# All 256 tokens turned before the first product, fp32r products as filler on TensorE, and high-part products first in the opening passes of a short-convolution layer

## The chip, the cores and the metric

The kernel runs on one core of one Trainium2 chip. The metric is the device time of one execution in microseconds (us), as the median of several runs. The engines are TensorE (PE; its weight loads are PEld), VectorE (DVE), ScalarE (ACT), GpSimd (POOL) and SyncE (SP), which issues most of the DMAs.

## What is computed

One layer for 256 tokens of width 2048, with a branch width of 4096, all in float32:

```python
h = rmsnorm(x, norm_g[0])                      # (1, 256, 2048)
mod = silu(c) @ ada_w[0] + ada_b[0]            # (1, 6144): shift, scale, gate
h = h * (1.0 + scale) + shift
proj = h @ w_in                                # (1, 256, 16384)
b_gate, c_gate, v, g = split(proj, 4)
u = causal_depthwise_conv(c_gate * v, conv_w)  # width 3
y = (b_gate * u * silu(g)) @ w_out             # (1, 256, 2048)
out = rmsnorm(x + gate * y, final_g)
```

The weights are large against the activations: `w_in` has 134 MB, `ada_w` 50 MB, `w_out` 34 MB, and each is read once.

## The kernel before, in words

**Precision.** A float32 product is made of three fp32r products: every operand is split into a high part (a cast to fp32r) and a low part (the rest), and high x high, high x low and low x high are added in PSUM. For a piece of `w_in` the split is a CAST `hi` on ACT (line 335) and a subtraction `lo` on DVE (line 336). For the features it is `hT`: its high half `hh_` is written on ACT (325), its low half `hl_` on DVE (326 and 329). The three products of a weight block are called 0 (hi, `hh_`), 1 (hi, `hl_`) and 2 (lo, `hh_`) in `product` (line 430 issues them all).

**Order of the input projection.** The 2048 input features are 16 slices k of 128. Features can be used only once their `shift` and `scale` are known, and these need all 16 rows of a piece of `ada_w`, so slices come in groups of two (`ADA = [2] * 8`). `plan()` writes down the order of the work: passes over a pair of 512-column chunks and one of four quarters of `w_in`, each with a range k0 to k1 of slices. The first passes use slices 0 and 1 alone (the opening passes, k0 = 0); later ones add more slices to the saved partial sums `acc`. A pass of 2 chunks and 2 slices loads 1 MB of `w_in`, is 48 products, and has one or two pieces of `ada_w` of 512 KB beside it. In this text P0 and P1 are the two first, half-wide passes (24 products each), and P2, P3 and so on are the passes behind them in the plan's order; the eighth opening pass, P8, takes slices 0 to 3. SP loads in the order of the plan: `raw_s` (line 478, three buffers) and `at` (399, four buffers). A finished bank goes to `acc` (451 on ACT, or 453 on DVE); a later pass may begin with a copy of `acc` back into its bank (465, a seed).

**The front.** `in_order()` pins the order on every engine, as traced, from the loads of `x` up to `pinned.close()`. x is loaded as four tiles `x00`, `x01`, `x10`, `x11` (128 tokens x 1024 columns). ACT and DVE make the sums of squares, `rstd` follows (281 to 283). `turn_x(0, 4)` scales the first 512 columns of x (ACT, 296 and 300), turns them on PE (eight transposes, 305) and copies them to `xs` on ACT (306). The first piece of `ada_w` (16 rows k, `first_ada`) is summed with `silu_c`: rows 7, 11 and 15 on PE (`ON_PE`, four products of 128 x 1 each, line 348), the others on DVE into `gv0` (359, 361), which a last product with ones adds up (`sum0(None, ...)`). `idle(n)` fills PE's waits with `IDLE` transposes of the identity matrix (251). `modulate` then makes `scale` and `shift` (320 to 322) and the features of slices 0 and 1.

**Behind the front.** The other twelve slices of x are turned in the middle of the opening passes: `turn_at` calls `turn_x` after the fourth, sixth and tenth saved partial sum, and with the first of these the convolution's weights are turned too (`turn(rows2, ...)`). In every chunk the products run block by block, with all three terms of a block together: high, high, low (`chunk_products`); the two first half-wide pieces alone go term by term (`late=True`). Outside the pinned front a scheduler places the instructions by its own estimate of time, so the order on an engine isn't the order of the code alone.

Of the kernel before, what the change touches and what calls it, by code (L numbers as in the profile page):

```python
# [8 lines left out]
F32 = mybir.dt.float32  # L9
F32R = mybir.dt.float32r  # L10
# [3 lines left out]
P = 128  # L14
D = 2048
E = 4096
T = 256
# [111 lines left out]
def short_conv_layer(ctx: ExitStack, tc: tile.TileContext, x, c, norm_g, ada_w, ada_b, w_in, conv_w, w_out, final_g, out):  # L129
# [69 lines left out]
    IDLE = (16, 30, 24, 14, 14, 6)  # L199
# [14 lines left out]
    for n, (j, kk) in enumerate(((0, 4), (4, 4), (8, 4), (12, 2), (14, 1), (15, 1))):  # L214
# [4 lines left out]
        if j == KT - 1:  # L219
            raw0 = raw_tile("raw0")  # L220
            first_load(raw0, 0)
# [3 lines left out]
    for k in range(1, NK0):  # L225
        first_load(raw0, k)
# [20 lines left out]
    tp_idle = psum.tile([P, CT, T], F32, tag="mm", name="tp_idle")  # L247

    def idle(n):
        for _ in range(n):  # L250
            nc.tensor.transpose(tp_idle[:, 0, 0:P], ident, ident)


# [4 lines left out]
    idle(IDLE[0])  # L258
# [4 lines left out]
    idle(IDLE[1])  # L263
# [15 lines left out]
    nc.vector.tensor_copy(vec, tp_v)  # L279
    nc.vector.tensor_scalar_add(b_scale1, vec[:, 32:48], 1.0)  # L280
# [11 lines left out]
    def turn_x(k0, k1, vector=False):  # L292

        c0, n = k0 % 8 * P, (k1 - k0) * P
        x0, x1 = (xt[t][k0 // 8][:, c0 : c0 + n] for t in range(TT))
        nc.scalar.activation(x0, x0, AF.Copy, scale=rstd[:, 0:1])
        if vector:
            nc.vector.tensor_scalar_mul(x1, x1, rstd[:, 1:2])
        else:
            nc.scalar.activation(x1, x1, AF.Copy, scale=rstd[:, 1:2])  # L300
        for i in range(0, k1 - k0, 2):
            tp = psum.tile([P, 2, T], F32, tag="sm", name="tp_x", bufs=2)
            for j in range(2):
                for t, xn in enumerate((x0, x1)):
                    nc.tensor.transpose(tp[:, j, t * P : (t + 1) * P], xn[:, (i + j) * P : (i + j + 1) * P], ident)  # L305
            nc.scalar.copy(xs[k0 // CT][:, k0 % CT + i : k0 % CT + i + 2, :], tp)
# [4 lines left out]
    def modulate(k0, nk, sums):  # L311
# [11 lines left out]
        for k in range(k0, k0 + nk):  # L323
            hf = xs[k // CT][:, k % CT, :]
            nc.scalar.activation(hh_[:, k], hf, AF.Identity, bias=shift[:, k : k + 1], scale=scale[:, k : k + 1])  # L325
            nc.vector.tensor_scalar(
                out=hf, in0=hf, scalar1=scale[:, k : k + 1], scalar2=shift[:, k : k + 1], op0=ALU.mult, op1=ALU.add
            )
            nc.vector.tensor_tensor(out=hl_[:, k], in0=hf, in1=hh_[:, k].bitcast(F32), op=ALU.subtract)
# [397 lines left out]
```

## Time and profile before

| | |
|---|---|
| median of 3 runs | 922.97 us (922.72 to 924.28) |
| profiled execution | 922.73 us |
| its span, first to last instruction | 921.0 us |
| around the span | 1.7 us |
| mean granted TensorE clock | 0.994 |
| PE busy | 905.1 us, 98% |
| DVE busy | 627.0 us, 68% |
| ACT busy | 450.3 us, 49% |
| moved by DMA | 227.64 MB, mean 247 GB/s |

A row of the timeline shows the start in us from the span's start, the length in us, the engine, the line, the operation, what it writes and reads, its shape and the number of instructions that were merged into it; in brackets stands the idle time of the engine before it, and who ended that. A row of the windows shows the length of a stretch and, for each engine, its busy time with the number of instructions, then the granted TensorE clock (1.00 is full), the busy share of the DMA engines and GB/s. The chain of waits is followed back from the last instruction to what released each step; its rows are start, length and what ran.

### The profile page before, as it was taken

The numbers are of one execution on the slowest core, as the hardware profiler recorded it, in microseconds if no ns is written. First come the engines' busy times: TensorE is split into PE (matmuls) and PEld (weight loads), VectorE is DVE, ScalarE is ACT, GpSimd is POOL, SyncE is SP. The second block draws the span as 40 slices with busy tenths as digits, with TensorE's granted clock in tenths as the row PEclk, the third lists the DMA queues.
The fourth block names the chain that finished last, engine by engine and source line by source line (L and its number), as shares of the span: only waits on it lengthen the run. The fifth ranks groups of instructions, "written<-read, shape, count | busy, mean of one in ns | idle before, by whom it ended". The sixth has DMA issues, their size and how long they took to land.

```text
span 921.0 us, 16348 instructions
## 1 busy us (share of the span) xinstructions
PE 905.1 (98%) x7119; PEld 871.3 (95%) x7119; DVE 627.0 (68%) x601; ACT 450.3 (49%) x427; POOL 0.7 (0%) x6
## 2 busy tenths in 40 slices
PE   7899999999999999999999999999999999999996
PEld 7899999999999999999999999999999988888885
DVE  5888898999875899986545544555454535555882
ACT  3778975545544755544443334433444333443333
POOL 0000000000000000000000000000000000000000
PEclk9899999999999999999999999999999999999999
DMA  9999999999995569867566656665666486565542
GB/s 313 368 382 357 344 336 360 342 348 344 353 347 200 184 214 353 276 209 229 186 200 200 192 185 194 203 198 184 191 188 201 142 330 229 192 205 195 184 137 91
DMA packets 147367, 227.64 MB, mean 247 GB/s; under 512 B 5424, under 2 KB 103904, under 8 KB 146912
## 3 DMA queue, kind: packets, MB, share of 16 engines
q1 hardware_dynamic: 147056, 226.51, 73.2%
q8 instruction: 55, 0.90, 0.4%
q10 hardware_dynamic: 240, 0.09, 0.0%
q14 instruction: 16, 0.13, 0.0%
HBM read 224.49 MB, written 2.10 MB: 246 GB/s over the span
## 4 chain that ended last, share of the span: by engine, by line
PE 95%; DMA 3%; SPq 1%; DVE 0%; ACT 0%; ACTq 0%; issue 0%; DVEq 0%
PE mm_b L430 38%; PE mm_s L430 37%; PE mm_o L625 6%; PE mm_o L626 6%; PE mm_o L624 6%; DMA at<-in_ada_w_dram 2%; DMA x<-in_x_dram 1%; DMA raw_s<-in_sc_w_in_dram 1%; PE ps_gate L563 0%; SPq L223 0%; PE tp_g L419 0%; PE tp_x L305 0%; DVE lo L336 0%; SPq L203 0%; SPq L399 0%; ACT big L643 0%
## 5 line engine op out<-in xcount | busy, mean ns | idle before, releaser
L430 PE MATMUL mm_s<-hT,hi 128*128 128x256 f32 x2048 | 353.0, 278 | 1.0 <-ACT hT L325 0.5
L430 PE MATMUL mm_b<-hT,hi 128*128 128x256 f32 x2048 | 348.8, 276 | 0.0
L430 PEld LDWEIGHTS mm_s<-hT,hi 128*128 128x128 f32 x2048 | 310.6, 189 | 2.1 <-ACT hT L325 0.7
L430 PEld LDWEIGHTS mm_b<-hT,hi 128*128 128x128 f32 x2048 | 308.3, 188 | 0.2 <-issue 0.2
L430 PE MATMUL mm_s<-hT,lo 128*128 128x256 f32 x1024 | 283.1, 278 | 1.8 <-DVE lo L336 1.8
L430 PE MATMUL mm_b<-hT,lo 128*128 128x256 f32 x1024 | 282.6, 276 | 0.0
L336 DVE TENSOR_TENSOR lo<-raw,hi 128x2048 fp32r<-128x2048 f32 (+1 forms) x66 | 148.0, 2243 | 128.1 <-ACT hi L335 128.1
L335 ACT CAST hi<-raw 128x2048 fp32r<-128x2048 f32 (+1 forms) x66 | 123.7, 1874 | 203.8 <-PE mm_b L430 149.9
L430 PEld LDWEIGHTS mm_s<-hT,lo 128*128 128x128 f32 x1024 | 192.9, 189 | 2.0 <-DVE lo L336 2.0
L430 PEld LDWEIGHTS mm_b<-hT,lo 128*128 128x128 f32 x1024 | 192.2, 188 | 0.2 <-issue 0.2
L335 ACT CAST hi<-raw_s 128x2048 fp32r<-128x2048 f32 (+1 forms) x64 | 121.6, 1901 | 102.6 <-PE mm_s L430 88.9
L336 DVE TENSOR_TENSOR lo<-raw_s,hi 128x2048 fp32r<-128x2048 f32 (+1 forms) x64 | 145.4, 2273 | 33.2 <-ACT hi L335 30.3
L336 DVE TENSOR_TENSOR lo<-raw_o,hi 128x2048 fp32r<-128x2048 f32 x32 | 73.3, 2291 | 66.1 <-ACT hi L335 66.1
L335 ACT CAST hi<-raw_o 128x2048 fp32r<-128x2048 f32 x32 | 61.0, 1907 | 106.9 <-PE mm_o L626 88.0
L625 PE MATMUL mm_o<-lo,y 128*128 128x512 f32 x256 | 99.7, 391 | 0.0
L624 PE MATMUL mm_o<-hi,y 128*128 128x512 f32 x256 | 99.3, 389 | 0.0
L626 PE MATMUL mm_o<-hi,y 128*128 128x512 f32 x256 | 99.3, 389 | 0.0
L412 DVE SCALAR_TENSOR_TENSOR gv<-at,silu_c,gv 128x512 f32<-128x512 f32 x105 | 78.5, 749 | 2.5 <-DMA at<-in_ada_w_dram 0.8
L625 PEld LDWEIGHTS mm_o<-lo,y 128*128 128x128 f32 x256 | 48.1, 188 | 10.1 <-issue 0.2
L626 PEld LDWEIGHTS mm_o<-hi,y 128*128 128x128 f32 x256 | 48.0, 188 | 10.1 <-issue 0.2
L624 PEld LDWEIGHTS mm_o<-hi,y 128*128 128x128 f32 x256 | 48.1, 188 | 10.0
L451 ACT COPY acc<-mm_s 128x1024 f32<-128x1024 f32 x43 | 43.5, 1014 | 18.1 <-PE mm_s L430 18.0
(94 smaller groups left out, 382.2 us busy)
## 6 DMA issues: line engine op xcount, KB each, us to landing
raw<-in_sc_w_in_dram SPq DMA_DIRECT2D x64, 1024.0 KB, 5.6
raw_s<-in_sc_w_in_dram SPq DMA_DIRECT2D x63, 1024.0 KB, 7.0
raw_o<-in_sc_w_out_dram SPq DMA_DIRECT2D x32, 1024.0 KB, 5.2
at<-in_ada_w_dram SPq DMA_DIRECT2D x114, 256.0 KB, 6.8
at_g<-in_ada_w_dram SPq DMA_DIRECT2D x32, 512.0 KB, 7.0
at<-in_ada_w_dram SPq DMA_DIRECT2D x6, 512.0 KB, 8.8
x<-in_x_dram SPq DMA_DIRECT2D x4, 512.0 KB, 6.1
big<-in_x_dram SPq DMA_DIRECT2D x2, 1024.0 KB, 9.6
```

The costliest lines, as they stand in the source:

```text
L335: nc.scalar.copy(hi[:, :n], raw[:, :n])
L336: nc.vector.tensor_tensor(out=lo[:, :n], in0=raw[:, :n], in1=hi[:, :n].bitcast(F32), op=ALU.subtract)
L412: nc.vector.scalar_tensor_tensor(out=gv, in0=at4[:, i], scalar=c_k, in1=gv, op0=ALU.mult, op1=ALU.add)
L430: mm = last_mm[0] = nc.tensor.matmul(dst, w, h[:, k], start=begins and left, stop=ends, skip_group_check=True)
L451: nc.scalar.copy(acc[ch, q], bank)
L624: nc.tensor.matmul(po, yh, hi[:, o], start=opens, stop=False, skip_group_check=True)
L625: nc.tensor.matmul(po, yh, lo[:, o], start=False, stop=False, skip_group_check=True)
L626: nc.tensor.matmul(po, yl, hi[:, o], start=False, stop=ct == NCT - 1, skip_group_check=True)
```

## The change

It has five parts.

1. All 16 slices are turned in the front: `scaled_x` and `turn_x` for four groups of four slices, into whole PSUM banks (`turned`), with one copy of 128 x 1024 each. The three later calls of `turn_x` and `turn_at` are gone. The convolution's weights are turned in the front as well (`tp_c`, `cw`).
2. `idle` issues fp32r products of 256 columns (a tile of ones, `ones_r`, that DVE fills) in place of transposes of 128 columns, in other numbers and places.
3. First sums: rows 3, 7, 11 and 13 on PE instead of 7, 11 and 15, between the turns.
4. Loads and casts: the first two pieces of `w_in` (`raw0`) are loaded behind all of `first_ada` instead of around its last row; their casts are made together on ACT ahead of the features, and the low parts on DVE in turn with `features(k)`. They share one `hi` and one `lo` tile.
5. `opening_products`: in passes with k0 = 0 the products with the high part of the weights (terms 0 and 1) of a chunk come first for all slices and blocks, and those with the low part (term 2) after them.

`plan()`, the loads' sizes and the number of products that count are the same.

```diff
-    IDLE = (16, 30, 24, 14, 14, 6)
+    IDLE = (20, 8, 28, 2, 6, 4, 12, 8)
...
-        if j == KT - 1:
-            raw0 = raw_tile("raw0")
-            first_load(raw0, 0)
...
-    for k in range(1, NK0):
+    raw0 = raw_tile("raw0")
+    for k in range(NK0):
         first_load(raw0, k)
...
+    turned = [psum.tile([P, CT, T], F32, tag="mm", name="tp_x") for _ in range(3)]
+    ones_r = slot([P, 2 * T], "ones_r", F32R)
+    nc.vector.memset(ones_r.bitcast(F32), 1.0)
+    def idle(n, where):
+        for _ in range(IDLE[n]):
+            nc.tensor.matmul(where[:, 0, :], ones_r[:, 0:P], ones_r[:, T:], start=True, stop=True, skip_group_check=True)
...
-    idle(IDLE[0])
+    idle(0, turned[2])
     tp_v = turn(rows1, 0, 64, None)
...
-    idle(IDLE[1])
+    idle(1, turned[2])
+    tp_c = turn(rows2, 0, 96, None)
+    idle(2, turned[2])
...
+    def scaled_x(j):
+        c = slice(j % 2 * CT * P, (j % 2 + 1) * CT * P)
+        for t in range(TT):
+            xp = xt[t][j // 2][:, c]
+            nc.scalar.activation(xp, xp, AF.Copy, scale=rstd[:, t : t + 1])
+    def turn_x(tp, j):
+        for i in range(CT):
+            c = slice((j % 2 * CT + i) * P, (j % 2 * CT + i + 1) * P)
+            for t in range(TT):
+                nc.tensor.transpose(tp[:, i, t * P : (t + 1) * P], xt[t][j // 2][:, c], ident)
...
-    ON_PE = (7, 11, 15)
+    ON_PE = (3, 7, 11, 13)
...
+    scaled_x(0)
+    scaled_x(1)
+    turn_x(turned[0], 0)
+    nc.scalar.copy(xs[0], turned[0])
+    sum0_of(0)
+    scaled_x(2)
+    turn_x(turned[1], 1)
+    nc.scalar.copy(xs[1], turned[1])
+    idle(3, turned[2])
+    sum0_of(1)
+    idle(4, turned[2])
+    scaled_x(3)
+    turn_x(turned[2], 2)
+    nc.scalar.copy(xs[2], turned[2])
+    turned.append(psum.tile([P, CT, T], F32, tag="mm", name="tp_x"))
+    idle(5, turned[3])
+    sum0_of(2)
+    turn_x(turned[3], 3)
+    nc.scalar.copy(xs[3], turned[3])
+    sum0_of(3)
+    tp_idle = psum.tile([P, CT, T], F32, tag="mm", name="tp_idle")
+    idle(6, tp_idle)
     sum0(None, gv0, ones[:, 0:1])
...
+    for k in range(NK0):
+        nc.scalar.copy(hi0[:, k * w : (k + 1) * w], raw0[:, k * w : (k + 1) * w])
+    for k in range(NK0):
+        c = slice(k * w, (k + 1) * w)
+        nc.vector.tensor_tensor(out=lo0[:, c], in0=raw0[:, c], in1=hi0[:, c].bitcast(F32), op=ALU.subtract)
+        features(k)
+    idle(7, tp_idle)
...
+    def opening_products(bank, hi, lo, w, o0, s0, sk, k1):
+        terms = [(i, m, t) for ts in ((0, 1), (2,)) for i in range(sk) for m in range(CT) for t in ts]
...
+                if first == 0:
+                    opening_products(bank, hi, lo, w, j * CT * P, s0, sk, k1)
...
-        if step[2] == 0 and turn_at and len(acc) >= turn_at[0]:
-            k = 16 - 4 * len(turn_at)
-            turn_at.pop(0)
-            with tc.issue_after(last_mm[0].ins), behind(ended):
-                turn_x(k, k + 4)
-                if k == 4:
-                    turn(rows2, 0, 96, cw)
```

The scheduler places the rest. Three places show it.

On ACT, from the first features to the cast of P2's weights, before (`raw0` is the weights of P0, `raw_s_352` of P1, `raw_s_392` of P2; lines 296 and 300 are the scaling of x for the later turns):

```order
L335 CAST hi_301<-raw0_113 128x512
L325 ACTIVATE hT_197<-xs0_198,shift_202,scale_203 128x256 x2
L335 CAST hi_320<-raw0_113 128x512
L335 CAST hi_354<-raw_s_352 128x1024
L296 ACTIVATE x00_84<-x00_84,rstd_186 128x512
L300 ACTIVATE x10_86<-x10_86,rstd_186 128x512
L296 ACTIVATE x01_85<-x01_85,rstd_186 128x512
L300 ACTIVATE x11_87<-x11_87,rstd_186 128x512
L296 ACTIVATE x01_85<-x01_85,rstd_186 128x512
L300 ACTIVATE x11_87<-x11_87,rstd_186 128x512
L335 CAST hi_394<-raw_s_392 128x2048
```

The same place on ACT now (`raw_s_376` is the weights of P1, `raw_s_416` of P2, `raw_s_486` of P3):

```order
L377 COPY xs2_217<-tp_x_132 128x1024
L382 COPY xs3_218<-tp_x_286 128x1024
L397 CAST hi_328<-raw0_115 128x512 x2
L337 CAST hi_378<-raw_s_376 128x1024
L327 ACTIVATE hT_214<-xs0_215,shift_219,scale_220 128x256 x2
L337 CAST hi_418<-raw_s_416 128x2048
L497 COPY acc01_373<-mm_s_348 128x1024
L497 COPY acc11_412<-mm_s_375 128x1024
L337 CAST hi_488<-raw_s_486 128x2048
```

The six scalings between the first features and P2's cast are gone from there, and the cast of P1's weights now stands ahead of the first features, not behind them.

On PE, the products of P2 (banks `mm_s_390` and `mm_s_391`), a part of its first chunk before:

```order
L430 MATMUL mm_s_390<-hT_197,hi_394 128x256 x2
L430 MATMUL mm_s_390<-hT_197,lo_395 128x256
L430 MATMUL mm_s_390<-hT_197,hi_394 128x256 x2
L430 MATMUL mm_s_390<-hT_197,lo_395 128x256
L430 MATMUL mm_s_390<-hT_197,hi_394 128x256 x2
L430 MATMUL mm_s_390<-hT_197,lo_395 128x256
```

P2 (banks `mm_s_414` and `mm_s_415`) and P3 (`mm_s_484` and `mm_s_485`) on PE now, whole:

```order
L465 MATMUL mm_s_414<-hT_214,hi_418 128x256 x16
L465 MATMUL mm_s_415<-hT_214,hi_418 128x256 x15
L465 MATMUL mm_s_414<-hT_214,lo_419 128x256 x8
L465 MATMUL mm_s_415<-hT_214,hi_418 128x256
L465 MATMUL mm_s_415<-hT_214,lo_419 128x256 x8
L465 MATMUL mm_s_484<-hT_214,hi_488 128x256 x16
L465 MATMUL mm_s_485<-hT_214,hi_488 128x256 x16
L465 MATMUL mm_s_484<-hT_214,lo_489 128x256 x8
L465 MATMUL mm_s_485<-hT_214,lo_489 128x256 x8
```

A pass used its low part from the third product on; now 31 or 32 products of the 48 come ahead of it.

On ACT, ahead of the features of slices 4 and 5 (`hT` from `xs1`, line 325 before and 327 now), which pass P12 is the first to use; `tp_g` with `gs` are the four sums that these features need, `mm_s<-acc` are seeds, `acc<-mm_s` saved banks. Before:

```order
L451 COPY acc11_388<-mm_s_991 128x1024
L421 ACTIVATE tp_g_1073,gs_1074<-tp_g_1073 128x128
L465 COPY mm_s_1142<-acc03_538 128x1024
L421 ACTIVATE tp_g_1073,gs_1074<-tp_g_1073 128x128 x2
L451 COPY acc02_456<-mm_s_1059 128x1024
L421 ACTIVATE tp_g_1073,gs_1074<-tp_g_1073 128x128
L465 COPY mm_s_1144<-acc13_540 128x1024
L335 CAST hi_1278<-raw_s_1276 128x2048
L465 COPY mm_s_1213<-acc00_622 128x1024
L325 ACTIVATE hT_197<-xs1_199,shift_202,scale_203 128x256 x2
```

Now, from the third of the four sums on:

```order
L337 CAST hi_1198<-raw_s_1196 128x2048
L511 COPY mm_s_1123<-acc13_547 128x1024
L456 ACTIVATE tp_g_1052,gs_1053<-tp_g_1052 128x128
L337 CAST hi_1257<-raw_s_1255 128x2048
L511 COPY mm_s_1192<-acc00_615 128x1024
L456 ACTIVATE tp_g_1052,gs_1053<-tp_g_1052 128x128
L497 COPY acc03_545<-mm_s_1121 128x1024
L497 COPY acc13_547<-mm_s_1123 128x1024
L511 COPY mm_s_1194<-acc10_617 128x1024
L511 COPY mm_s_1321<-acc21_680 128x1024
L327 ACTIVATE hT_214<-xs1_216,shift_219,scale_220 128x256 x2
```

Two saved banks and two more seeds, one of them for pass P13, now stand between the last of the four sums and these features.

More of the change, by code (lines that the diff above doesn't have):

```diff
@@ L366, in short_conv_layer @@
+    idle(7, tp_idle)
     pinned.close()
-    with behind(ended):
-        for k in range(1, NK0):
-            pieces0.append(split(raw0[:, k * CT * P : (k + 1) * CT * P], CT * P))
+    pieces0 = [(hi0, lo0)]
     def conv(ct, u, cv):
@@ L467, in parts @@
             for k in range(NK0):
-                chunk_products(banks[0], *pieces0[k], 0, k, k0, k1, late=True)
+                chunk_products(banks[0], *pieces0[0], k * CT * P, k, k0, k1, late=True)
             pieces0.clear()
```

68 lines of the change are left out of this document (32 added, 36 removed).

## The prediction

> **What bounds the kernel now.** I read the page first, then the chain of waits for the first 70 us, then windows and timeline around its gaps.
>
> ```profile
> span 921.0 us, 16348 instructions
> PE 905.1 (98%) x7119; PEld 871.3 (95%) x7119; DVE 627.0 (68%) x601; ACT 450.3 (49%) x427; POOL 0.7 (0%) x6
> ```
>
> PE is busy for 98% of the span, so time is won only where PE waits, runs at a lower clock, or does work that isn't the reference's. The chain says where that is (start, length, what):
>
> ```profile
> 20.09 5.69 DMA raw_s<-in_sc_w_in_dram
> 34.89 2.29 DVE lo L336
> 37.23 6.77 PE mm_s L430 x44
> 44.00 0.87 PE tp_x L305 x8
> 44.88 2.97 PE mm_s L430 x26
> 50.51 0.87 PE tp_x L305 x8
> 51.38 10.92 PE mm_s L430 x96
> 62.30 0.87 PE tp_x L305 x8
> ```
>
> Until 37.23 us the end hangs on loads and on one low part, from there on PE. A product takes 10.92 / 96 = 0.114 us, 48 of them 5.46 us. P2 ends at 44.00, P3 starts at 44.88 behind a turn, and two more turns follow. So the question is when P3 can start, and what PE still does besides products after it.
>
> The clock in the gaps (length, PE busy with count, clock, DMA share, GB/s):
>
> ```profile
> 19.86:23.27 3.41, 2.69 (x25) 1.00 1.05 363
> 23.27:26.69 3.42, 2.73 (x23) 1.00 0.96 324
> 26.69:30.10 3.41, 3.41 (x16) 0.50 1.01 355
> 33.51:36.93 3.42, 1.44 (x8) 1.00 1.02 405
> 36.93:40.34 3.41, 3.11 (x14) 0.50 1.06 367
> 40.34:43.75 3.41, 3.41 (x32) 1.00 1.09 374
> ```
>
> Two stretches of 3.41 us run at half clock, with 14 and 16 products where a full one holds 30 (3.41 / 0.114). Each lies behind a stretch with little streamed on PE. DMA is full throughout: a load lands when the bytes ahead of it have passed, and the change alters neither bytes nor, up to P3's weights, their order to speak of.
>
> The timeline of P2 and P3 before:
>
> ```profile
> 25.97 1.09 ACT L325 ACTIVATE hT<-xs,shift,scale 128x256 fp32r<-128x256 f32 x2 [2.14 <-DVE shift L322]
> 27.48 1.04 ACT L335 CAST hi<-raw_s 128x1024 fp32r<-128x1024 f32 x1
> 28.43 0.72 ACT L296 ACTIVATE x<-x,rstd 128x512 f32<-128x512 f32 x1
> 32.12 1.89 ACT L335 CAST hi<-raw_s 128x2048 fp32r<-128x2048 f32 x1
> 37.23 0.58 PE L430 MATMUL mm_s<-hT,lo 128*128 128x256 f32 x1 [1.76 <-DVE lo L336]
> 37.36 1.90 ACT L335 CAST hi<-raw_s 128x2048 fp32r<-128x2048 f32 x1 [1.53 <-DMA raw_s<-in_sc_w_in_dram]
> 39.29 2.29 DVE L336 TENSOR_TENSOR lo<-raw_s,hi 128x2048 fp32r<-128x2048 f32 x1 [0.66 <-ACT hi L335]
> 39.94 1.91 ACT L335 CAST hi<-raw_s 128x2048 fp32r<-128x2048 f32 x1 [0.68 <-DMA raw_s<-in_sc_w_in_dram]
> 56.78 1.92 ACT L335 CAST hi<-raw_s 128x2048 fp32r<-128x2048 f32 x1 [1.53 <-PE mm_s L430]
> ```
>
> P2's cast stood behind six scalings of x (28.43 to 32.1), its low part came at 37.2, and PE needed it from the third product on. P3's cast (37.36) and P4's (39.94) waited for their loads. By 56.78 the cast waits for PE: the loads are ahead.
>
> **The change, part by part.** *Start of the first product.* The front's rows:
>
> ```profile
> 8.73 5.57 PE L251 MATMUL tp_idle<-ident 128*128 128x128 f32 x30
> 12.58 0.72 ACT L296 ACTIVATE x<-x,rstd 128x512 f32<-128x512 f32 x1 [0.23 <-DVE rstd L283]
> 14.14 1.04 PE L305 MATMUL tp_x<-ident,x 128*128 128x128 f32 x8
> 15.02 2.78 PE L251 MATMUL tp_idle<-ident 128*128 128x128 f32 x24
> 17.64 0.95 PE L348 MATMUL sum<-silu_c,at 128*128 128x1 f32 x8
> 19.44 4.69 DVE L361 SCALAR_TENSOR_TENSOR gv<-at,silu_c,gv 128x512 f32<-128x512 f32 x6 [0.69 <-DMA at<-in_ada_w_dram]
> 24.38 1.03 PE L348 MATMUL sum<-ones,gv 128*128 128x1 f32 x8
> 29.18 1.22 DVE L336 TENSOR_TENSOR lo<-raw_s,hi 128x1024 fp32r<-128x1024 f32 x1
> ```
>
> The sums in `gv0` end at 24.13 (six steps from 19.44) and still are six: row 13 goes to PE, row 15 comes to DVE, whose load is no longer behind `raw0`. PE must now do, from the first turn at about 14.3 (rstd 0.2 later for the copy to `cw`), 32 transposes (4 x 1.04), four groups of sums (4 x 0.95) and 24 fillers (0.114 each, 2.7): 10.7 us, to about 25.0; transposes and sums overlap at their seams (14.14 + 1.04 runs to 15.18, the next starts at 15.02), which gives 24.5 to 25.0. The sum with ones takes it to 25.5 to 26.0, `scale` and `shift` 0.45 more. But on ACT the cast of P1's weights is now ahead of the features. Its load landed at 25.78 (20.09 + 5.69) and the cast takes 1.04, so the features begin at 26.85 instead of 25.97, and the first product comes at about 27.45 instead of 26.62: 0.85 later, by ACT, which covers PE's lateness. ACT's own front, eight scalings (0.72) and four copies (1.0) from 12.8 to about 23, fills time in which it lay idle. So do the fill of `ones_r` on DVE near 1 us, whose first long step waits for x until 8.9, and the turn and copy for `cw`, while x lands. If that cover were gone, they would cost 0.2 to 0.4 us each on a chain with 0.9 us to spare.
>
> *P0 and P1.* On DVE the low part of P1 (1.22) also goes ahead: `hl_` of slice 0 at 28.9, of slice 1 at 30.4. PE issues nine products, waits 0.4 us for the first, and the 48 products end at about 27.45 + 5.46 + 0.5 = 33.4.
>
> *P2.* Between its load and P3's lie 2.6 MB, 7.0 us at 372 GB/s, so it ended near 37.36 - 7.0 = 30.3; with no scaling ahead the cast runs 30.3 to 32.2 and the low part to about 34.8 behind some sums. 31 high products (3.5 us) come first, so the low part is needed at 36.9. P2 runs 33.4 to 38.9, without the 1.76 us wait.
>
> *P3.* The cast can't end before 37.36 + 1.90 = 39.26, since the load doesn't move. Low part by 41.6, needed at 42.9. So P3 starts at 39.26 instead of 44.88: **5.6 us**. This is the cap: a front up to 0.4 us faster or slower changes nothing, and each us beyond counts. P4 (cast from 39.94 on, needed at 44.7) and the passes behind it are fed, since a pass with one and a half pieces of `ada_w`, 1.84 MB, takes 4.9 us at 372 GB/s (PE 5.46), and low parts lie in the shade of 16 to 32 high products. The price of that order: a pass's first bank ends 8 products before the pass, not 24, and its copy (1.0) must be done 2.7 us later, when the next pass opens its second bank. One cast ahead of it on ACT fits, two don't; I put it at nothing while casts have come early, and at up to 1 us a pass if not.
>
> *The turns behind the front.* Two more of 0.87 us and the turn of the convolution's weights (0.08, estimated from PE's gap between 44.88 + 2.97 and the next products) leave PE's dense stretch: **1.8 us**. Their copies leave ACT, whose idle time covered them.
>
> *New waits behind.* The features of slices 4 and 5 move on ACT behind two saved banks and two seeds.
>
> ```profile
> 66.92 0.30 ACT L421 ACTIVATE tp_g<-tp_g 128x128 f32<-128x128 f32 x1
> 96.58 1.02 ACT L465 COPY mm_s<-acc 128x1024 f32<-128x1024 f32 x1
> 97.52 1.92 ACT L335 CAST hi<-raw_s 128x2048 fp32r<-128x2048 f32 x1
> 100.28 1.09 ACT L325 ACTIVATE hT<-xs,shift,scale 128x256 fp32r<-128x256 f32 x2
> 103.66 0.75 DVE L329 TENSOR_TENSOR hT<-xs,hT 128x256 fp32r<-128x256 f32 x2
> ```
>
> Before, the low features were there at 104.4 (103.66 + 0.75). Counted on from P3's start, PE has made the four sums' transposes (half a turn, 0.44, as in the group before) by 39.26 + 407 x 0.114 + 0.9 = 86.5, and reaches P12's second half, 528 products on, at 100.1. From 86.5 ACT has seven copies (0.94, a row less the 0.08 by which rows overlap), two casts (1.84), four sums (0.4 with their read-out) and the features (0.5 each): the first stand at 98.9 and 99.4, and DVE's low half, with a sum of `gv` between (0.7), at about 100.6. PE waits 0.4 us. Bounds: 0 if that sum slips behind, 1.0 if ACT is one copy later. I take **0.4 lost**, nearest to the walk.
>
> Sum: 5.6 + 1.8 - 0.4 = 7.0 us. On the profiled execution that is 922.73 - 7.0 = 915.7; the median stands 0.24 above it, so 916.0. Bounds: 7.5 (no new wait) and 6.4 (1.0 there), 915.4 to 916.6.
>
> **The rivals.** *One or two half-clock stretches in P0 to P2.* The grid of 3.41 us doesn't hang on the kernel's own steps. Behind 24 us some placements of it hold only the filler and few products: 26.4 to 27.45 and 28.5 to 28.9 are empty, and the sum with ones (1.03 us of one-column products) streams nearly nothing. The same windows for these sums alone:
>
> ```profile
> 19.86:23.27 3.41, 0.95 (x8) 0.97 (x8) 0.00 (x0) 1.00 1.05 363
> 23.27:26.69 3.42, 1.95 (x16) 1.86 (x16) 0.31 (x2) 1.00 0.96 324
> ```
>
> Without them, 1.44 and 2.73 - 1.95 = 0.78 us of busy time led to half clock, and 2.69 - 0.95 = 1.74 didn't; the changed front can fall to about 1.3. One stretch costs 14 products, 1.6 us, less the 0.4 that P3's cap hides: 917.2; two 918.8. For it: both half-clock rows. Against it: eight fillers before P0 and no gap over 1.1 us. The Trainium skill, in "TensorE: Matmul & The Clock Gate", Part 1, has the clock fall only after an idle window of about 3.4 us; by that rule this rival is out and 916.0 stands. The trace disagrees: PE's longest wait ahead of the second half-clock row was 1.76 us.
>
> *Slower: the front's PE chain at half clock.* Transposes and one-column sums fill PE from 14.3 to 24.5. At half clock a transpose takes 5.57 / 30 = 0.186, a filler 0.22 (3.11 / 14), a sum group 0.95 to 1.9: the chain ends at 29.4 to 33, the first product comes at 32 to 36, P3 12.5 us later (96 products and one half-clock stretch). It turns slower where the first product is later than 33.8, since P3 then passes 46.3 (44.88 + 1.8 - 0.4). At 35.5 it gives 924.7. Against it: 30 transposes took 5.57 and the next 24 only 2.78, so transposes alone brought the full clock. The Trainium skill, in "TensorE: Matmul & The Clock Gate", Part 4, says that transposes don't count as busy work for the clock; by that this rival would be the forecast, 924.7, and the trace disagrees by those two rows.
>
> *Given back later.* ACT's order changes up to about 110 us, and waits like that at P12 could add up to 3 us more: 919.0. For it: the late banks, and ACT's full queue ahead of P12. Against it: casts wait for PE by 56.78, not for loads.
>
> *No gain.* The passes behind P3 turn out bound by loads, or the change's fillers hold the last sum up by 7 us, so that it doesn't do what it says: 923.0. The DMA share of over 1.0 speaks for it, the row at 56.78 against it.
>
> **How the numbers follow.** Forecast 0.47, half clock 0.30, given back 0.10, no gain 0.06, slower 0.07. The range of 8 in 10 takes the forecast and the half-clock cases whole and most of what is given back: 915.0 (0.4 under the best sum, for the scatter of 922.72 to 924.28) to 918.9. This kernel's times can't tell less than about 0.2% (1.8 us) from no change. Faster 0.87, same 0.06, slower 0.07.
>
> **What would show it.** P3's cast released by its load near 37.4 and P3's first product near 39.3; no PE wait on `lo`; first product at 27.4 with P1's cast ahead of the features; no turns behind 27 us; a wait near 100 us under 1 us. I am wrong if P3 starts after 41 without half clock, if its load lands elsewhere, or if PE waits over 1 us behind 45.

## The result, and the profile after

The changed kernel takes 915.98 us in the median of five runs (915.44 to 916.12), against 922.97 us (920.96 to 924.28) for the kernel before: a ratio of 0.9924, with a 95% interval of 0.9912 to 0.9936. The profiled execution took 916.12 us, 6.61 less than the one before. The page of the changed kernel gives span and busy times:

```profile
span 914.3 us, 16328 instructions
PE 900.3 (98%) x7111; PEld 866.4 (95%) x7111; DVE 627.2 (69%) x601; ACT 449.7 (49%) x423; POOL 0.7 (0%) x6
```

PE is 4.8 us less busy, for one because nothing runs at half clock behind 8.04 us; the rest of the 6.7 us is waiting that went. The chain of waits, changed kernel (start, length, what):

```profile
24.73 1.07 PE sum L349 x8
28.59 9.23 DMA raw_s<-in_sc_w_in_dram
37.93 1.92 ACT hi L337
39.89 16.62 PE mm_s L465 x144
56.51 0.44 PE tp_g L454 x4
56.94 29.82 PE mm_s L465 x263
```

Before, the chain passed a low part at 34.89, 44 products behind it and three turns. Now it goes from P3's load over P3's cast straight into PE, which is not left again up to the sums of the next features. The same stretch in the timeline, PE, ACT and DVE:

```profile
26.27 1.05 ACT L337 CAST hi<-raw_s 128x1024 fp32r<-128x1024 f32 x1 [0.85 <-DVE shift L392]
27.22 1.09 ACT L327 ACTIVATE hT<-xs,shift,scale 128x256 fp32r<-128x256 f32 x2
27.86 0.73 PE L465 MATMUL mm_s<-hT,hi 128*128 128x256 f32 x4 [1.02 <-ACT hT L327]
30.84 1.92 ACT L337 CAST hi<-raw_s 128x2048 fp32r<-128x2048 f32 x1 [2.54 <-DMA raw_s<-in_sc_w_in_dram]
33.12 2.28 DVE L338 TENSOR_TENSOR lo<-raw_s,hi 128x2048 fp32r<-128x2048 f32 x1
33.96 3.68 PE L465 MATMUL mm_s<-hT,hi 128*128 128x256 f32 x31
37.47 1.07 PE L465 MATMUL mm_s<-hT,lo 128*128 128x256 f32 x8
37.93 1.91 ACT L337 CAST hi<-raw_s 128x2048 fp32r<-128x2048 f32 x1 [2.75 <-DMA raw_s<-in_sc_w_in_dram]
39.89 3.92 PE L465 MATMUL mm_s<-hT,hi 128*128 128x256 f32 x32 [0.33 <-ACT hi L337]
```

P2 begins at 33.96, makes its high parts' products without a stop, and its low part, there at 35.40 (33.12 + 2.28), is used at 37.47. P3 waits 0.33 us for its cast, which waited for its load. The longer waits of PE from 26 to 112 us are few, in the waits of the changed kernel (total, times, longest):

```profile
PE mm_s L465 <- ACT hT L327: 1.0, 1, 1.0
PE mm_s L465 <- ACT hi L337: 0.3, 1, 0.3
PE mm_s L465 <- DVE hT L331: 0.2, 1, 0.2
```

The first is P0's wait for the features of slice 0, the last P1's for the low features of slice 1; no turn and no low part is among them. The new wait foretold for P12 is too short for a row here, but DVE shows it. The low features of slices 4 and 5 in the timeline:

```profile
100.63 0.42 DVE L331 TENSOR_TENSOR hT<-xs,hT 128x256 fp32r<-128x256 f32 x1
...
101.62 0.42 DVE L331 TENSOR_TENSOR hT<-xs,hT 128x256 fp32r<-128x256 f32 x1
```

They were ready at 101.05 and 102.04, and PE began the half that uses them at 100.77.

The experiments are read with one table, from the trace of one execution of each kernel: the start in us of the n-th product of the input projection. Product 0 opens P0, 48 opens P2, 96 P3, 144 P4. In the changed kernel 384 is the first to use slices 2 and 3, and 624 the first to use slices 4 and 5, in P12's second half, which is done by 672; in some of the other kernels the scheduler mixes that half with its neighbours, and there 624 and 672 are marks of progress alone. Every ratio below is to the kernel before, timed in the same set of runs. No two kernels differ by more than 0.3 us in what lies behind product 1000, except the two with the loads spread.

| kernel | 0 | 48 | 96 | 144 | 384 | 624 | 672 | 1000 |
|---|---|---|---|---|---|---|---|---|
| before | 26.62 | 34.07 | 44.63 | 51.14 | 79.83 | 107.52 | 112.96 | 150.63 |
| changed | 27.86 | 33.96 | 39.89 | 45.46 | 73.11 | 100.77 | 106.48 | 144.15 |
| changed, once more | 27.73 | 35.03 | 40.68 | 46.33 | 74.00 | 101.66 | 107.36 | 145.02 |
| before, order of products alone | 26.89 | 34.32 | 40.67 | 46.71 | 75.89 | 103.59 | 109.03 | 146.66 |
| changed, old order of products | 26.78 | 32.95 | 39.68 | 47.14 | 74.83 | 102.52 | 107.96 | 145.63 |
| features first | 26.80 | 32.88 | 40.60 | 46.17 | 73.83 | 101.48 | 106.92 | 144.55 |
| P3's load early | 27.75 | 33.84 | 39.28 | 45.76 | 73.78 | 101.44 | 107.66 | 145.28 |
| both of these | 26.60 | 32.16 | 37.59 | 45.11 | 72.88 | 100.58 | 106.83 | 144.46 |
| transposes as filler | 27.46 | 34.53 | 39.97 | 45.47 | 73.12 | 100.78 | 108.42 | 146.06 |
| no last fillers | 27.85 | 35.14 | 40.58 | 46.02 | 73.67 | 102.21 | 107.65 | 145.28 |
| late low features | 27.77 | 34.95 | 40.39 | 45.83 | 73.48 | 101.14 | 106.58 | 144.21 |
| loads spread | 26.71 | 32.88 | 38.33 | 43.77 | 71.65 | 103.09 | 109.90 | 149.59 |
| loads spread, features first | 26.85 | 32.44 | 37.88 | 43.32 | 74.47 | 109.04 | 114.48 | 152.11 |

Of the 6.7 us in the span, 4.74 are there at P3's first product (44.63 less 39.89; the first two products of P3 stood ahead of the turn before, so that its dense part began at 44.88 and the gain is 4.99 there), 6.72 at product 384, and 0.27 is given back in P12's second half (5.71 us for 48 products instead of 5.44).

### The profile page after: what moved, and what is told of

Read it like the earlier page. It is cut to its first block, busy times and chain, and to the rows that moved or that the text cites. A ratio compares the mean times of both kernels' runs of the same rounds, so it can differ in the third digit from the quotient of the medians.

```text
span 914.3 us, 16328 instructions
## 1 busy us (share of the span) xinstructions
PE 900.3 (98%) x7111; PEld 866.4 (95%) x7111; DVE 627.2 (69%) x601; ACT 449.7 (49%) x423; POOL 0.7 (0%) x6
## 4 chain that ended last, share of the span: by engine, by line
PE 95%; DMA 3%; DVE 1%; ACT 1%; SPq 0%; issue 0%; ACTq 0%; DVEq 0%
PE mm_b L465 38%; PE mm_s L465 37%; PE mm_o L666 6%; PE mm_o L667 6%; PE mm_o L665 6%; DMA raw_s<-in_sc_w_in_dram 1%; DMA at<-in_ada_w_dram 1%; DMA x<-in_x_dram 1%; DVE gv L363 1%; PE ps_gate L604 0%; PE tp_g L454 0%; ACT hi L337 0%; SPq L220 0%; DVE lo L338 0%; PE sum L349 0%; SPq L203 0%
## 5 line engine op out<-in xcount | busy, mean ns | idle before, releaser
L465 PE MATMUL mm_s<-hT,hi 128*128 128x256 f32 x2048 | 337.0, 277 | 1.6 <-ACT hT L327 1.0
L465 PEld LDWEIGHTS mm_s<-hT,hi 128*128 128x128 f32 x2048 | 299.3, 188 | 2.8 <-ACT hT L327 1.2
L465 PE MATMUL mm_s<-hT,lo 128*128 128x256 f32 x1024 | 262.1, 276 | 0.0
L338 DVE TENSOR_TENSOR lo<-raw,hi 128x2048 fp32r<-128x2048 f32 x64 | 146.7, 2292 | 128.8 <-ACT hi L337 128.7
L337 ACT CAST hi<-raw 128x2048 fp32r<-128x2048 f32 x64 | 122.4, 1913 | 197.2 <-PE mm_b L465 149.9
L465 PEld LDWEIGHTS mm_s<-hT,lo 128*128 128x128 f32 x1024 | 182.8, 188 | 0.0
```

What stands on the lines that cost most here:

```text
L337: nc.scalar.copy(hi[:, :n], raw[:, :n])
L338: nc.vector.tensor_tensor(out=lo[:, :n], in0=raw[:, :n], in1=hi[:, :n].bitcast(F32), op=ALU.subtract)
L465: mm = last_mm[0] = nc.tensor.matmul(dst, w, h[:, k], start=begins and left, stop=ends, skip_group_check=True)
```

## The experiments

**The order of the products alone, in the kernel before.** All else stays as before: the front, the turns between the passes, the scalings ahead of P2's cast.

```diff
+                if first == 0:
+                    opening_products(bank, hi, lo, w, j * CT * P, s0, sk, k1)
+                else:
```

> The kernel before with one part of the change alone: P2, P3 and the other opening passes make their high parts' products first; scalings, turns, casts and fillers stay as they were. Theory (the wait for the low part set P3's start, not the scalings ahead of P2's cast): P2 begins where it began, near 34.1, runs 48 products dense without the 1.76 us wait and without the half-clock stretch behind it, to 39.5; a turn of 0.87 follows, P3 begins at 40.4 instead of 44.88, and the time falls by some 4.5 us, to 918.5. Rival (the scalings and turns in ACT's order are what held P2 and P3, as the prediction told it): only the 1.76 us wait goes, 921.2.

Measured: 918.86 us (918.46 to 919.13), ratio 0.9958 (0.9945 to 0.9970); 4.0 us earlier at product 1000. PE in the timeline of this kernel:

```profile
34.32 3.91 PE L430 MATMUL mm_s<-hT,hi 128*128 128x256 f32 x32 [1.57 <-ACT hi L335]
38.07 1.98 PE L430 MATMUL mm_s<-hT,lo 128*128 128x256 f32 x16
39.88 1.04 PE L305 MATMUL tp_x<-ident,x 128*128 128x128 f32 x8
40.67 3.44 PE L430 MATMUL mm_s<-hT,hi 128*128 128x256 f32 x28
```

P2 begins where it began, with its cast still behind the scalings and PE waiting 1.57 us for it, and the 48 products run through; P3 comes at 40.67 behind its turn. The theory holds as far as this: without the wait for the low part at the third product, and the half clock that followed that wait, P3 comes 4 us earlier although the scalings stay. The next run shows that the scalings had a part in P3's lateness too.

**The old order of the products, in the changed kernel.** The reverse of the first experiment: the front and the casts of the change, `chunk_products` in all passes.

```diff
-                if first == 0:
-                    opening_products(bank, hi, lo, w, j * CT * P, s0, sk, k1)
-                else:
-                    for i in range(sk):
+                for i in range(sk):
```

> The changed kernel without one part of the change: the opening passes make their products in the old order, so that a low part is needed at the third product. Theory: P2 waits from its third product for its low part at 35.4 (1.2 us, mostly hidden by P3's cap), P3 waits for its low part at 42.16, so that it runs as if begun at 41.9 instead of 39.89; the later passes are fed, so about 2.0 us are lost, 918.0, and up to 1.6 more if a half-clock stretch follows the waits. Rival (the turns in the front are the gain, and the cap hides the order): 916.0, as the changed kernel.

Measured: 919.07 us (917.67 to 919.64), ratio 0.9956 (0.9942 to 0.9970); the profiled execution, at 917.70, is 1.5 us behind the changed kernel at product 1000. Waits of PE from 26 to 112 us:

```profile
PE mm_s L465 <- DVE lo L338: 2.0, 2, 1.6
```

P2's low part, in the timeline of DVE:

```profile
31.63 2.29 DVE L338 TENSOR_TENSOR lo<-raw_s,hi 128x2048 fp32r<-128x2048 f32 x1
```

It was done at 33.92 and cost 0.41 us instead of 1.76 in the kernel before; so with the scalings and turns gone, P3 came at 39.68 in the old order too. P3's low part cost 1.6, and P4 began at 47.14 instead of 45.46. The theory holds in kind: 1.5 us lost in this execution, 2.0 expected, and 3.1 between the medians (2.1 against the changed kernel's second five runs). The two parts overlap: by product 1000 the order alone gives 4.0 us (150.63 less 146.66), the rest without it 5.0, both together 6.5. Four of the six runs of this kernel took 1.2 us or more longer than the profiled one. P3's load landed at 36.95 here, 0.9 us earlier than in the changed kernel's profiles; a later landing in the other runs could be a part of that, but their loads weren't seen.

**Features ahead of P1's cast.** In the changed kernel P1's cast and low part go behind the features of slices 0 and 1.

```diff
+            if chs == (1,) and first == 0:
+                with behind(ended):
+                    hi, lo = split(raw, n)
+            else:
+                hi, lo = split(raw, n)
```

> The changed kernel with P1's cast behind the features of slices 0 and 1 on ACT, and its low part behind them on DVE. Theory of the cap (P3's load and cast set P3's start): the first product comes at 26.9 instead of 27.86 and P2 ends 0.9 earlier, but P3 still waits for its cast, which ends near 39.8: PE then waits about 1.2 us there instead of 0.33, and the time is 915.7 to 916.0. Rival (PE's chain sets P3, and the cap is no cap): the whole 0.9 us is gained, 915.1.

Measured: 917.60 us (915.72 to 918.40), ratio 0.9943 (0.9927 to 0.9959). The first product came 1.06 us earlier, P2 began 1.08 earlier, and P3 0.71 later than in the changed kernel. ACT in the timeline:

```profile
37.74 1.01 ACT L497 COPY acc<-mm_s 128x1024 f32<-128x1024 f32 x1 [3.08 <-PE mm_s L465]
38.65 1.90 ACT L337 CAST hi<-raw_s 128x2048 fp32r<-128x2048 f32 x1
```

P3's load had landed at 37.93, but the scheduler had put the copy of P2's first bank ahead of the cast, so that PE waited 2.0 us there instead of 1.2. So an earlier start of the passes is lost at P3, as the cap says, but here the copy held the cast beside the load. The median is 1.6 us over the 916.0 that the theory allowed; the profiled execution, at 916.52, shows only 0.4 of that at product 1000.

**P3's load ahead of the pieces of `ada_w`.** In the changed kernel the four pieces that are traced up to P2's pass come behind P3's load. Every later piece is also tied behind the load of `w_in` traced before it, which is a second, smaller change.

```diff
+            if last_load:
+                tc.add_manual_dep(dma.ins, last_load[0].ins.name, after, reason="behind the load")
...
+    held = [p for s in steps[:3] for some in s[-1] for p in some]
+    for s in steps[:3]:
+        s[-1][:] = [[] for _ in s[-1]]
+    steps[3][-1][0][:0] = held
```

> The changed kernel with P3's load issued ahead of the pieces of ada_w that stood between it and P2's load (2 MB then stand between P3's load and P4's); the features stay behind P1's cast. Theory of the cap: P3's load lands near 34 instead of 37.83, PE's wait of 0.33 us at P3 goes, and no more, since P2 ends at 39.56: 915.7. Rival one (P3's load was the end of a chain worth several us): 914 or less. Rival two: P4's load, now later, becomes the cap and 0.5 to 1.5 us are lost, 916.5 to 917.5.

And with the features first as well:

> The changed kernel with P1's cast behind the features, and with P3's load issued ahead of the pieces of ada_w that stood between it and P2's load. Theory of the cap: with the cap gone P3 begins when P2 ends, near 38.7 instead of 39.89, and some 1.2 us are gained, 914.8, unless P4's load, now behind 2 MB of ada_w, comes to be the next cap (it must be cast by 44.2; I expect its landing near 41.8 and its cast done at 43.8). Rival (the load is not what P3 waits for): the same as with the features first alone.

Measured: 916.88 us (916.41 to 917.29), ratio 0.9942 (0.9929 to 0.9954), for the early load; 916.75 us (916.09 to 917.19), ratio 0.9935 (0.9922 to 0.9948), for both. The casts of P3 and P4 on ACT, first with the load early, then with both:

```profile
33.80 1.91 ACT L337 CAST hi<-raw_s 128x2048 fp32r<-128x2048 f32 x1 [0.44 <-DMA raw_s<-in_sc_w_in_dram]
43.80 1.91 ACT L337 CAST hi<-raw_s 128x2048 fp32r<-128x2048 f32 x1 [3.30 <-DMA raw_s<-in_sc_w_in_dram]
```

```profile
33.40 1.92 ACT L337 CAST hi<-raw_s 128x2048 fp32r<-128x2048 f32 x1 [1.73 <-DMA raw_s<-in_sc_w_in_dram]
43.16 1.90 ACT L337 CAST hi<-raw_s 128x2048 fp32r<-128x2048 f32 x1 [1.63 <-DMA raw_s<-in_sc_w_in_dram]
```

P3's load came 4 us earlier and P3 began at 39.28 and 37.59, when P2 ended. That is what the cap says. But P4's cast now waited for its load until 43.80 and 43.16 (41.55 in the changed kernel), and of the 2.30 us that P3 had gained with both edits 0.35 were left at P4 and 0.23 at product 384. Rival two of the first expectation is right, with 0.3 us lost at P4 and 1.1 by product 1000 (145.28 less 144.15); of these, 0.5 came between products 624 and 672. P4's load landed at 43.08 with both edits, 1.3 us behind the 41.8 that I had put there.

**The loads spread.** So that no single load is late, the pieces of `ada_w` were spread: none between P2's and P3's load, then one, then two a pass, and the same number by P9; the tie of pieces to loads stays. This and the next kernel also hold the order of the run with late low features, further down.

```diff
+    counts = (0, 0, 0, 1, 2, 2, 2, 2, 4)
+    held = [p for s in steps[: len(counts)] for some in s[-1] for p in some]
+    for s, n in zip(steps, counts):
+        s[-1][:] = [held[:n]] + [[] for _ in s[-1][1:]]
+        del held[:n]
```

> The order of products of the run with late low features, and the pieces of ada_w spread otherwise: none between the loads of P2 and P3, one between those of P3 and P4, two between P4 and P5, and the same total by P9. Theory: no load is a cap any more (P3 lands near 33.7, P4 near 38, P5 near 43); P3 then begins when P2 ends, 39.3 as in the run with P3's load early, and P4's and P5's waits of that run (0.5 us each) go: 0.6 us less than the changed kernel with late low features, 915.1. Rival (the bytes are only owed: a later load is late by what an earlier one gained): no gain, 915.7 or more.

> The run with the loads spread, and P1's cast behind the features of slices 0 and 1. Theory: with no load as cap, the first product's 1.0 us (26.8 instead of 27.8) now counts whole up to P3 and behind it: 914.1, 1.0 below the run with the loads spread, where the same step gained nothing without the spreading. P3 begins near 37.8. Rival (another cap, casts on ACT or low parts on DVE, takes the place of the loads): 915.0 or more.

Measured: 925.97 us (922.74 to 926.82), ratio 1.0024 (1.0010 to 1.0038), and 928.72 us (926.39 to 932.69), ratio 1.0063 (1.0046 to 1.0080). Beside the run with late low features (915.55), whose order they share, that is 10.4 and 13.2 us more. Both theories fell; the first rival, that the bytes are only owed, fits, though it foresaw nothing of this size. The beginning went as expected: P3 at 38.33 and 37.88, P4 at 43.77 and 43.32, and no wait for a load up to there. Then it was paid back several times over. Waits of PE from 26 to 250 us, loads spread, then with the features first:

```profile
PE mm_s L468 <- ACT mm_s L514: 3.2, 2, 1.7
PE mm_s L468 <- DVE hT L331: 1.6, 3, 1.1
```

```profile
PE mm_s L468 <- ACT hT L327: 3.3, 1, 3.3
PE mm_s L468 <- DVE hT L331: 2.7, 1, 2.7
```

In the first kernel PE waited 1.1 us for the low features of slices 4 and 5, and twice for a seed (line 514 here) that stood behind other work on ACT. In the second the features of slices 2 and 3 came too late, both the high and the low ones, and the clock was half from 75.36 to 82.19. These features need sums of `ada_w`, the pieces that the spreading put off; the front's 2 us are owed to them. Whether the spreading or the tie of each piece to a load did most of it stays open.

**Fillers as transposes.** In the changed kernel `idle` issues transposes of the identity again, in the new numbers and places.

```diff
-            nc.tensor.matmul(where[:, 0, :], ones_r[:, 0:P], ones_r[:, T:], start=True, stop=True, skip_group_check=True)
+            nc.tensor.transpose(where[:, 0, 0:P], ident, ident)
```

> The changed kernel with every filler product in the front (fp32r, 128x256) replaced by a transpose of the identity, as before the change, in the same number. Theory: the clock comes to full speed later, near 13 us as before instead of 8.04, which only lengthens the second filler run and the first turn, by up to 1.4 us; ACT's cast of P1's weights, which waits for its load, sets the first product, so little of it is left: 916.0 to 916.5, if the run-up to P0 keeps the clock. Rival one: the transposes stream too little and one or two stretches of P0 to P2 run at half clock, 917.2 to 918.8. Rival two, by the rule in the Trainium skill, TensorE: Matmul & The Clock Gate, Part 4, that transposes don't count as busy work: the front stays at half clock, the first product comes at 32 to 36 and the time is above 920.

Measured: 918.43 us (917.37 to 919.86), ratio 0.9960 (0.9946 to 0.9973), 2 us more than expected, but not in the front. A window of this kernel, then DVE and PE in its timeline around P12:

```profile
27.29:30.70 3.41, 3.24 (x15) 3.25 (x16) 3.34 (x7) 0.61 (x2) 0.00 (x0) 0.50 1.01 365
```

```profile
98.73 2.33 DVE L447 SCALAR_TENSOR_TENSOR gv<-at,silu_c,gv 128x512 f32<-128x512 f32 x3
100.97 2.28 DVE L338 TENSOR_TENSOR lo<-raw_s,hi 128x2048 fp32r<-128x2048 f32 x1
...
105.14 0.76 DVE L331 TENSOR_TENSOR hT<-xs,hT 128x256 fp32r<-128x256 f32 x2
...
103.31 0.39 PE L465 MATMUL mm_s<-hT,lo 128*128 128x256 f32 x1 [1.92 <-DVE lo L338]
```

The clock was full from 10.22 us on and then half for this one stretch, and P2 began 0.57 later; P3 was 0.08 later, the rest of it hidden by the cap. The 1.94 us came at products 624 to 672. PE's order is another one there: the program puts P13's first products, on slices 2 and 3, ahead of most of P12's second half, whose low features came only at 105.90 (105.14 + 0.76) here. P13's low part was done at 103.25, behind three sums of `gv`, and PE waited 1.92 us for it; the changed kernel begins at this place with P12's second half, whose low part had been done at 96.38. Only the front's fillers had been edited; the order on PE and DVE 75 us later is what the scheduler made of it. So this run says little against or for the fillers' time, and it shows what P12's place can cost.

**Without the last fillers.**

```diff
-    IDLE = (20, 8, 28, 2, 6, 4, 12, 8)
+    IDLE = (20, 8, 28, 2, 6, 4, 0, 0)
```

> The changed kernel without its last two runs of fillers (12 before the sum with ones, 8 behind it); nothing else is changed. PE then has between about 22.8 and 27.9 us only that sum, 1.05 us of one-column products. Theory (the clock falls by what is streamed in a stretch of 3.41 us, as in both half-clock rows of before): one stretch in P0 to P2 runs at half clock, 1.6 us later at P2's end, of which P3's cap hides 0.33: 917.2, with 917.0 to 918.9 if it falls twice. Rival (by the Trainium skill, TensorE: Matmul & The Clock Gate, Part 1, it takes an idle window of about 3.4 us, and no wait here is longer than about 2): the clock stays full and the time is 916.0.

Measured: 917.56 us (916.81 to 918.44), ratio 0.9951 (0.9937 to 0.9965). Windows of this kernel (length, PE busy with count, PEld, DVE, ACT, POOL, clock, DMA share, GB/s), then the sums' share of the first:

```profile
21.34:24.76 3.42, 1.57 (x13) 1.32 (x11) 2.57 (x4) 1.60 (x2) 0.00 (x0) 1.00 0.81 260
24.76:28.17 3.41, 1.70 (x8) 1.61 (x9) 1.83 (x5) 2.55 (x5) 0.00 (x0) 0.50 0.95 320
28.17:31.58 3.41, 3.41 (x17) 3.41 (x17) 3.31 (x8) 0.65 (x2) 0.00 (x0) 0.50 1.05 376
```

```profile
21.34:24.76 3.42, 1.45 (x11) 1.32 (x11) 0.00 (x0) 1.00 0.81 260
```

Two stretches at half clock; P2 begins 1.18 us later and P3 0.69. The theory holds: two stretches, and a median inside the 917.0 to 918.9 that it gave for two. The first of them lies nearly all ahead of the first product (27.85) and so cost little. The rule of the Trainium skill, "TensorE: Matmul & The Clock Gate", Part 1, that the clock falls after an idle window of about 3.4 us, doesn't hold here: PE had 13 instructions and 1.57 us of work in the window ahead.

**More fillers in the kernel before.**

```diff
-    IDLE = (16, 30, 24, 14, 14, 6)
+    IDLE = (16, 30, 24, 14, 14, 10)
...
+    idle(8)
     sum0(None, gv0, ones[:, 0:1])
```

> The kernel before with more fillers behind the last sums (18 transposes instead of 6, 8 of them ahead of the sum with ones), so that the stretch from 26.69 to 30.10 need not run at half clock; nothing else is changed. Theory: half clock there cost nothing, since P2's cast, which ends at 34.0 behind ACT's scalings, sets P2's start: 922.5 to 923.0, unless the second half-clock stretch goes with it. Rival (each half-clock stretch costs its 1.6 us): 921.4.

Measured: 922.50 us (920.67 to 923.05), ratio 0.9999 (0.9991 to 1.0008). The number is the theory's, but the run doesn't test it:

```profile
24.88:28.29 3.41, 3.41 (x19) 3.41 (x18) 0.39 (x3) 0.09 (x1) 0.00 (x0) 0.50 1.00 363
28.29:31.70 3.41, 3.41 (x18) 3.41 (x17) 2.80 (x7) 3.41 (x6) 0.00 (x0) 0.50 1.09 360
```

The half clock came earlier and held for two stretches, the first product came at 29.52, 2.9 us later, and P3 at 44.62, as before, since P2 now ran at full clock. It is inconclusive.

**The changed kernel once more, and with late low features.** The second of these changes the order in all passes behind the opening ones:

```diff
-                        chunk_products(bank, hi, lo, i * w + j * CT * P, s0 + i, first, k1, seed)
+                        chunk_products(bank, hi, lo, i * w + j * CT * P, s0 + i, first, k1, seed, late=True)
```

> The changed kernel itself once more, beside the kernels of this call, since chips differ and the differences sought are about 1 us. Theory (all its runs are of one kind): within 0.5 us of 916.0. Rival (its wait at P12's features is sometimes longer, or a half-clock stretch sometimes falls into P0 to P2): some of its runs near 917.5 to 918.

> The changed kernel with another order of products in all passes behind the first nine: for each slice the high and low parts of w_in with the high part of h first, and only then the high part with the low part of h, so that the low features are needed at the ninth product of a slice instead of the second. Theory: the wait at P12's second half (0.27 us in the trace) goes, 915.7, and with it the danger that it grows. Rival: the wait there isn't for the low features but for ACT or a low part of w_in (needed at the fifth product instead of the third now), and the time stays 916.0.

Measured, on one chip: 917.00 us (916.27 to 917.22), ratio 0.9928 (0.9915 to 0.9941), for the changed kernel; 915.55 us (915.02 to 916.08), ratio 0.9916 (0.9903 to 0.9929), with late low features. The ranges of the two don't meet, the intervals do. So the changed kernel itself lies 1.0 us over its 916.0 here, between the theory's 916.5 and the rival's 917.5. Windows ahead of and at P0, first in the first profile of the changed kernel, then in the second:

```profile
25.11:28.52 3.41, 2.39 (x20) 2.19 (x20) 2.17 (x6) 2.35 (x4) 0.00 (x0) 1.00 0.98 302
28.52:31.93 3.41, 3.16 (x28) 2.97 (x27) 3.30 (x8) 1.09 (x1) 0.00 (x0) 1.00 1.06 374
```

```profile
24.77:28.18 3.41, 2.18 (x17) 1.98 (x18) 1.97 (x5) 2.55 (x4) 0.00 (x0) 1.00 1.00 347
28.18:31.60 3.42, 3.42 (x19) 3.42 (x18) 3.32 (x8) 0.76 (x1) 0.00 (x0) 0.50 1.06 365
```

The same program, the grid of 3.41 us 0.3 us earlier, and one stretch with 19 instructions instead of 28. It cost 1.07 us at P2, 0.79 at P3 and 0.87 in the span (915.2 against 914.3). So the half-clock rival is real: of the two profiled executions of the changed kernel, it fell on one.

With late low features, P12's second half took 5.44 us instead of 5.71 (5.70 in the second profile of the changed kernel). Its profile has a half-clock stretch at P0 as well (27.98 to 31.39), so the two are compared alike. The theory holds: with the low features needed seven products later, the loss there is gone. Beside the 0.26, 0.52 us came up to P12 (0.29 by P3, the rest at P4); why was not tried. This is the fastest version measured.

## Why the prediction was right, and where it was off

The forecast was 916.0 us and the result 915.98; on the profiled executions 7.0 was forecast and 6.61 came. The mechanism is the one told, P3 capped by its load and the turns gone from PE, but that the medians agree to 0.02 us is luck: P3 gained 0.6 less than told, the median of the changed kernel lay 0.14 below its profiled execution where that of the kernel before lay 0.24 above, and five more runs gave 917.00. The steps:

- *First product, P0, P1.* As told: P1's cast stood ahead of the features on ACT, the sum with ones ran 24.73 to 25.80, within the 25.5 to 26.0 told for its end. The first product came at 27.86 instead of 27.45, since P1's load landed at 26.11 instead of 25.78, and P1 ended 0.6 us later than 33.4.
- *P2 without its wait.* Right: low part at 35.40, needed at 37.47. The reason given for P2's lateness, the cast behind six scalings, is only a part of it: with the scalings left in place the order of the products alone took P3 from 44.63 to 40.67, and with the scalings gone and the old order P3 came at 39.68. Either is nearly enough for P3; the prediction added both to one sum and didn't say that they overlap.
- *P3 by its load.* Right in kind, 5.0 us instead of 5.6. The mis-sized step is "the load doesn't move": it landed at 37.83 instead of 37.28. In the second profile of the changed kernel it landed at 37.82, but with the old order of products, behind the same front and the same loads, at 36.95, so the delay doesn't come with the change each time. It arises ahead of P2's load, which was already 0.57 late (30.82 instead of 30.25). x had landed 0.55 later in the first profile (9.44, against 8.89 before), but only 0.16 later in the second, so that isn't all of it; what else delays the loads was not found. The 0.4 us of room ahead of the cap was 0.33.
- *The turns.* 1.8 told. From P3 to product 624 the gain grew from 4.99 to 6.75, by 1.76.
- *P12's features.* 0.4 told, 0.27 measured in each profile of the changed kernel. The sum's upper bound of 7.5 should read 7.4 (5.6 + 1.8).
- *The half-clock rival* was given 0.30 and 1.2 us. It is in the second profile, at 0.87 us. I had 14 products lost to a stretch; but at full clock that stretch holds 28 instructions, since P1 waits 0.25 us in it, and 19 were left: 9 x 0.114 = 1.03 us, less the 0.33 of room at P3. The forecast met the first five runs and was 1.0 us under the second five, on another occasion; of each only one execution shows when its clock fell (the mean clocks are 0.997 to 0.998 and 0.996 to 0.997), so I can't say that the half clock makes all of that difference.
- *The slower rival* is out: the clock was full from 8.04 us to 909.16, behind PE's last work. With transposes as filler it was full from 10.22 us, when PE had done nothing but transposes, so the Trainium skill's remark that transposes don't count ("TensorE: Matmul & The Clock Gate", Part 4) isn't borne out here.
- *Given back later* didn't come in the changed kernel, but the mechanism exists: 1.9 us at P12 with nothing but other fillers, and 10 to 13 us where the loads were spread (925.97 and 928.72 against 915.55).
- *No gain* is out: PE waited for no load behind P3.

## What to carry to other kernels

When an operand is split into a high part that is ready early and a low part that is ready late, let the first passes, which run on the heels of their loads, do all work on the early part first: that order alone was worth 4.0 of 6.5 us here. Gains of this kind overlap: with the rest of the change in place the same order added 1.5 us, since the rest alone gave 5.0. Before moving a load forward, look what its bytes push back: 2.3 us won at P3 were 0.2 us a few passes later, and with the pieces for later features held back they became a loss of 10 to 13 us. And where a scheduler orders the code, an edit at the front can move a wait 75 us further on, so compare the traces in progress marks to the end, not only at the place of the edit.

## What the runs showed of the hardware

- In every profile here the granted clock changes only on a grid of 3.41 us, whose place differs from execution to execution (25.11 and 24.77 in two profiles of one program). The Trainium skill has this window as free-running, in "TensorE: Matmul & The Clock Gate", Part 1, and the traces agree.
- Ahead of the half-clock stretches listed here lay a window with little streaming, and no idle time as long as the window: PE's longest pause in these was 1.85 us, without the last fillers. PE's busy time less that of the one-column sums was 2.18 - 0.67 = 1.51 us in the window ahead of the half clock of the changed kernel's second profile, 0.12 without the last fillers (1.57 - 1.45), and 1.44 and 0.78 in the two rows before the change. With 2.39 - 0.67 = 1.72 it stayed full. The sums alone, in the first and in the second profile of the changed kernel:

```profile
25.11:28.52 3.41, 0.67 (x7) 0.59 (x6) 0.31 (x2) 1.00 0.98 302
```

```profile
24.77:28.18 3.41, 0.67 (x6) 0.58 (x6) 0.31 (x2) 1.00 1.00 347
```

- The border isn't sharp by this measure. From 14.87 to 18.28 us in the first profile of the changed kernel it was 1.53 (3.41 less 1.88 of sums), and the clock stayed full. In the kernel with the order of the products alone, 1.73 us of transposes led to half clock and 1.84 us of products didn't:

```profile
10.98:14.39 3.41, 1.73 (x15) 1.30 (x13) 2.12 (x8) 1.63 (x3) 0.00 (x0) 1.00 1.10 350
...
31.46:34.87 3.41, 1.84 (x16) 1.64 (x15) 3.30 (x5) 3.41 (x4) 0.00 (x0) 1.00 1.06 391
```

- The clock was first full at 8.04 and 7.71 us in the changed kernel's profiles and at 13.03 in the one of before; but with transposes as filler at 10.22, and at 7.56 and 7.81 in two kernels with the front of before (order of the products alone, more fillers). So the fillers' kind doesn't decide it alone.
